# A two-layer recurrent trunk on one core: factors of a triangular inverse kept in half a PSUM bank, output transposes by two, sample states through the merge's banks

## The chip, the cores and the metric

The kernel runs on one core of a Trainium2 chip. The metric is the device time of one execution in microseconds. Five engines work beside one another: TensorE (PE in the profile: matmuls and transposes into PSUM; its weight loads are PEld), VectorE (DVE), ScalarE (ACT), GpSimd (POOL) and SyncE (SP, which here only issues DMAs). SBUF holds the tiles, PSUM has banks of 128 partitions by 512 floats, into which PE writes and from which DVE and ACT read.

## What is computed

A trunk of two layers over a prompt of 1024 tokens and 8 samples of 8 tokens, width 1024. Layer 0 is a gated linear recurrence, layer 1 a recurrence of the RWKV-7 kind with 16 heads of 64; each layer also attends to a memory, gates, projects back and adds to the residual. The part that the change touches is the recurrence of layer 1, whose reference is this step over time:

```python
def step(S, inp):
    r_t, w_t, k_t, v_t, a_t, b_t = inp
    sa = jnp.einsum('bhij,bhj->bhi', S, a_t)
    S = S * w_t[:, :, None, :] + sa[..., None] * b_t[:, :, None, :] + v_t[..., None] * k_t[:, :, None, :]
    y = jnp.einsum('bhij,bhj->bhi', S, r_t)
    return S, y
```

Its result is normalized by head, a bonus `(r*k).v` is added, and the prompt's and the samples' last states are outputs.

## The kernel before, in words

All arithmetic is in 32 bits. Up to about 1600 us of the profiled execution come layer 0, its output projection and the input projection of layer 1; from about 2170 us on the output projection of layer 1 runs. Between them lies the recurrence of layer 1.

It is computed in nine blocks: eight of 128 prompt tokens and one that holds the 64 tokens of all samples. `RSEQ` gives their order, 0, samples, 1, 2 ... 7. Each block is an object of class `Blk` with these stages:

- `pre` and `score_steps`: scaled keys (tiles `BKz`, `AR`; DVE and POOL), their products on PE (`psc`), masked by DVE into the tile `Q`.
- `tokens` and `values`: the keys turned by PE (`pbk`) and copied to `BKt`, and the value rows loaded.
- `inverse` (L1524 to L1562): within a block, tokens depend on one another through a unit triangular matrix of every head. ACT copies its diagonal parts of 16 by 16 to `Ld`, DVE transposes them (`Lu`) and adds two halves to the factors `L16` (L1549, the tile prints as `L`). Then fifteen steps of a substitution run on DVE, each a product `pd<-Xc,L` (L1553) of t by t elements in a partition and a sum `Xc<-pd` (L1554). Each step needs the one ahead of it. The result goes to `XN` and `XP`.
- `merge_steps` (L1564 to L1609): five rounds of 32 by 32 matmuls (`pn`, `px`, `py`, L1579) that put the inverses of 16 together to those of 64, with copies by DVE and ACT between them.
- `chain` (L1641 on): the recurrence itself. It starts from the state `S` (`chain<-S,AR`, L1669), goes through `W` and `UV`, and leaves the next state (`chainS`, L1719 to L1725). One block's chain needs the state of the one ahead.
- `out` (two groups `k`, each `out_group`, L1780 on): normalization by ACT, DVE and POOL, four transposes of `yv` on PE into one PSUM tile `pyt` (L1818), and copies with a bias to `oT` by ACT (L1821), then a DMA to `mixT`.
- `sample_in` for the samples' block: eight pairs of heads, each with a load of the states, transposes into PSUM (`ps`, L1621), a copy `S0T` (L1622), and two groups of sixteen products (`pas`, L1636) with a copy `AS` each (L1638). `sample_out` writes the samples' last states, two PSUM tiles a pair (`psn`, L1769, and `pec`, L1776).

The loop over the blocks says for block n: its chain; the merge of n+1 woven with the scores of n+2 (`WV` says how many steps of each in turn); the inverse and tokens of n+2; one or more pairs of `sample_out`; `pre` of n+3; `out` of n-1. Ahead of the loop two lists, `PLAN` and `PLAN2`, give the order of the last gate projections (g0 to g11), memory heads (x, s) and the first blocks' stages (p, c, t, i, m with a block's number). All this is a program order alone: a scheduler then places each instruction on its engine's queue by that order and its own simulated times, and adds the waits.

Three PSUM pools matter: two banks `psi` for the merge's tiles, one bank `psn` that `ps`, `pas`, `psn`, `pec` and `pyt` share one after the other, and three banks `psg` for the chain.

Of the kernel before, what the change touches and what calls it, by code (L numbers as in the profile page):

```python
# [9 lines left out]
F32 = mybir.dt.float32  # L10
F32R = mybir.dt.float32r
I32 = mybir.dt.int32
AF = mybir.ActivationFunctionType
# [30 lines left out]
    "x0 g0 x2 x1 g1 x3 s0 g2 g3 s1 g4 g7 p0 g5 c0 s2 s3", "t0 i0 m0 p1 g6 g8 g9 g10 g11")]  # L44
# [3 lines left out]
WV = (3, 8)  # L48
# [937 lines left out]
def rwkv_layer(ctx, g, nn, left):  # L986
# [252 lines left out]
    g.psi, g.psn = pool_ps("psinv", 2), pool_ps("pssmp", 1)  # L1239
    P["b"] = pS.enter_context(pool(g, "rb", 1))  # L1240
# [8 lines left out]
    with pool(g, "rl", 1, "right") as rl, pool(g, "sm2", 2, "right") as g.sm2:  # L1249
# [23 lines left out]
        for n, x in enumerate(seq):  # L1273
            if n == SIN:
                smp.sample_in()
            x.chain()
            ops(n + 1, "values")
# [106 lines left out]
class Blk:  # L1384
# [140 lines left out]
    def inverse(self):  # L1525
# [22 lines left out]
        L16 = self.tile("L16", "L16", 16, 16)  # L1548
# [61 lines left out]
    def sample_state(self, p):  # L1610
# [4 lines left out]
        ps = g.psn.tile([128, NB, 64], F32, name="ps0", tag="n")  # L1615
# [9 lines left out]
    def sample_in(self):  # L1625
# [4 lines left out]
        for p in range(8):  # L1630
            S0T = self.sample_state(p)
            o = HV[p // 4]
            for h in range(2):
                ps = g.psn.tile([128, 2, NB, LS], F32, name="pas", tag="n")
                for bb in range(NB):
                    nc.tensor.matmul(ps[o, :, bb, :], S0T[HV[h], bb, :], self.AR[p // 4][HV[h], p % 4, :2, LS * bb:LS * bb + LS],  # L1636
                                     start=True, stop=True)
                nc.scalar.activation(self.AS0[o, p % 4, h], ps[o].rearrange("p a b t -> p (a b t)"), AF.Copy)  # L1638
# [116 lines left out]
    def sample_out(self, pairs):  # L1755
# [3 lines left out]
        for p in pairs:  # L1759
# [4 lines left out]
            ps = g.psn.tile([128, NB, 64], F32, name="psn", tag="n")  # L1764
# [10 lines left out]
            ps = g.psn.tile([128, NB, 64], F32, name="pec", tag="n")  # L1775
# [9 lines left out]
    def out_group(self, k, last):  # L1785
# [30 lines left out]
        pt = g.psn.tile([128, 4, 128], F32, name="pyt", tag="n")  # L1816
        for j in range(4):
            nc.tensor.transpose(pt[:, j, :n], yv[:n, j], g.ident[:n, :n])  # L1818
        for j in range(4):
            for r, ts in halves:  # L1820
                nc.scalar.activation(oT[:, j, ts.start - self.t0:ts.stop - self.t0], pt[:, j, r], AF.Identity,  # L1821
                                     bias=vcol(g, "lb", 4 * k + j))
# [8 lines left out]
FILL = [[("x", 0)], [("x", 1)], [("x", 2)], [("x", 3), ("s", 0)], [("s", 1), ("s", 2), ("s", 3)], [("s", 4), ("s", 5), ("s", 6), ("s", 7)], [], [("g", 9), ("g", 8), ("g", 10), ("g", 11)]]  # L1831
# [39 lines left out]
```

## Time and profile before

| | us |
|---|---|
| median of 3 executions | 2331.82 |
| lowest and highest | 2329.45, 2335.67 |
| the profiled execution | 2339.18 |
| its span in the trace | 2337.4 |
| PE busy in the span | 2178.2 (93%) |
| DVE busy | 1326.3 (57%) |
| ACT busy | 1004.1 (43%) |
| POOL busy | 697.2 (30%) |

The profiled execution was 7.4 us longer than the median of the three others, and 1.8 us of it lie outside the span. A share over the whole span is a mean of stages with different limits. The views used below are cut to the stages: busy time by stretch, one line's durations, waits by engine, and the timeline.

### The profile page before, as it was taken

To read this page: it belongs to the slowest core of one execution; us is meant where nothing else is said; L and a number is where in the kernel's file an instruction comes from. 1 tells how busy PE (TensorE), PEld (TensorE's weight loads), DVE (VectorE), ACT (ScalarE), POOL (GpSimd) and SP (SyncE) were. 2 spreads that over 40 slices of the span, in tenths; PEclk is the share of its full clock that TensorE was granted. 3 is DMA by queue.
4 is the path that set the end of the run, shared out by engine and by line. 5 is a ranking of instruction groups with operands and counts; after the bars stand their busy time and mean duration, and the time that the engine had idled before them with its cause. 6 is when DMAs were issued, how large, how long until landed. Compare 5 with 4: busy or idle time off the path is not lost. (4 is left out here: it accounts for less than half of the span.)

```text
span 2337.4 us, 50528 instructions
## 1 busy us (share of the span) xinstructions
PE 2178.2 (93%) x20945; PEld 1956.6 (84%) x20945; DVE 1326.3 (57%) x2596; ACT 1004.1 (43%) x2244; POOL 697.2 (30%) x561
## 2 busy tenths in 40 slices
PE   5999999999999979989989999899999999998997
PEld 5989888887878858878979998898888888888786
DVE  6134666657776553375795313334666689875633
ACT  4223444444444442266554312444544545455411
POOL 3101122122122310044563412112233355546432
PEclk9999999999999989999989998999997799889999
DMA  5136122123431363215434424235432234314653
GB/s 188 62 101 172 49 73 66 46 63 102 115 94 57 101 218 115 76 48 198 151 132 156 126 95 138 60 81 152 123 113 76 58 90 117 94 52 126 188 156 100
DMA packets 360504, 253.00 MB, mean 108 GB/s; under 512 B 120570, under 2 KB 326594, under 8 KB 360274
## 3 DMA queue, kind: packets, MB, share of 16 engines
q1 hardware_dynamic: 348226, 237.66, 34.1%
q0 software_dynamic: 2544, 7.64, 1.0%
q10 hardware_dynamic: 9504, 4.46, 0.7%
q8 instruction: 165, 2.70, 0.5%
q14 instruction: 65, 0.53, 0.1%
HBM read 172.59 MB, written 77.11 MB: 107 GB/s over the span
## 5 line engine op out<-in xcount | busy, mean ns | idle before, releaser
L199 POOL TENSOR_TENSOR wlo<-wraw,whi 128x1024 fp32r<-128x1024 f32 (+1 forms) x88 | 199.0, 2269 | 569.7 <-ACT whi L196 532.7
L217 PE MATMUL pg<-hi,whi 128*128 128x288 f32 (+3 forms) x800 | 268.8, 336 | 3.4 <-DVE qk L611 3.3
L218 PE MATMUL pg<-lo,whi 128*128 128x288 f32 (+3 forms) x800 | 265.3, 332 | 0.0
L219 PE MATMUL pg<-hi,wlo 128*128 128x288 f32 (+3 forms) x800 | 262.4, 328 | 0.0
L196 ACT ACTIVATE whi<-wraw 128x1024 fp32r<-128x1024 f32 (+1 forms) x104 | 102.6, 993 | 162.6 <-issue 67.9
L217 PEld LDWEIGHTS pg<-hi,whi 128*128 128x128 f32 x800 | 153.2, 191 | 18.7 <-DVE qk L611 4.2
L218 PEld LDWEIGHTS pg<-lo,whi 128*128 128x128 f32 x800 | 153.2, 191 | 11.1 <-issue 1.6
L219 PEld LDWEIGHTS pg<-hi,wlo 128*128 128x128 f32 x800 | 152.9, 191 | 10.5 <-issue 1.0
L903 PE MATMUL pout<-owh,bh 128*128 128x512 f32 (+1 forms) x432 | 142.8, 399 | 13.0 <-ACT owh L196 13.0
L903 PE MATMUL pout<-owh,bl 128*128 128x512 f32 (+1 forms) x432 | 141.4, 396 | 2.1 <-DVE bl L199 2.1
L903 PE MATMUL pout<-owl,bh 128*128 128x512 f32 (+1 forms) x432 | 142.6, 396 | 0.0
L217 PE MATMUL pg<-xhi,whi 128*128 128x384 f32 (+2 forms) x392 | 128.0, 327 | 7.7 <-DVE evs L1147 5.0
L219 PE MATMUL pg<-xhi,wlo 128*128 128x384 f32 (+2 forms) x392 | 126.4, 322 | 0.0
L218 PE MATMUL pg<-xlo,whi 128*128 128x384 f32 (+2 forms) x392 | 125.7, 321 | 0.0
L903 PEld LDWEIGHTS pout<-owh,bh 128*128 128x128 f32 (+1 forms) x432 | 79.2, 184 | 33.9 <-ACT owh L196 13.2
L196 ACT ACTIVATE bh<-br 128x512 fp32r<-128x512 f32 (+1 forms) x54 | 32.1, 605 | 161.0 <-POOL br L872 75.2
L199 DVE TENSOR_TENSOR bl<-br,bh 128x512 fp32r<-128x512 f32 (+1 forms) x54 | 47.5, 880 | 94.0 <-ACT bh L196 94.0
L689 DVE TENSOR_TENSOR qk<-qk,tot 128x512 f32<-128x512 f32 (+1 forms) x96 | 83.0, 865 | 29.7 <-PE plev L717 18.5
L903 PEld LDWEIGHTS pout<-owh,bl 128*128 128x128 f32 (+1 forms) x432 | 79.1, 183 | 23.7 <-DVE bl L199 2.5
L243 PE MATMUL pg<-xhi,whi 128*128 128x384 f32 (+1 forms) x408 | 97.3, 335 | 0.0
L903 PEld LDWEIGHTS pout<-owl,bh 128*128 128x128 f32 (+1 forms) x432 | 79.3, 184 | 21.0 <-issue 0.4
L243 PE MATMUL pg<-xhi,wlo 128*128 128x384 f32 (+1 forms) x408 | 96.6, 334 | 0.0
(457 smaller groups left out, 6000.2 us busy)
## 6 DMA issues: line engine op xcount, KB each, us to landing
wraw<-in_w_in_dram SPq DMA_DIRECT2D x72, 512.0 KB
oraw<-in_w_out_dram SPq DMA_DIRECT2D x24, 512.0 KB
wraw<-in_w_mem_kv_dram SPq DMA_DIRECT2D x16, 512.0 KB
gT<-evs SPq DMA_DIRECT2D x12, 544.0 KB
vv<-vtk SPq DMA_DIRECT2D x24, 256.0 KB
br<-brT SPq DMA_DIRECT2D x24, 256.0 KB
gt<-gT SPq DMA_DIRECT2D x24, 256.0 KB
br<-mixT SPq DMA_DIRECT2D x24, 256.0 KB
```

Of the source, the lines that this page charges most:

```text
L196: nc.scalar.activation(hi, src, AF.Copy)
L199: (nc.gpsimd if elo == "pool" else nc.vector).tensor_sub(lo, src, hi.bitcast(F32))
L217: nc.tensor.matmul(out, ah, bh, start=first, stop=False)
L218: nc.tensor.matmul(out, ah, bl, start=False, stop=False)
L219: nc.tensor.matmul(out, al, bh, start=False, stop=last)
L243: nc.tensor.matmul(z[:, :n], a[:, k], x(k)[:, t0:t0 + n], start=first, stop=last)
L689: nc.vector.tensor_tensor(v, v, w[:, :, :, None].to_broadcast([128, 2, n // (2 * h), h]), op=ALU.mult)
L903: nc.tensor.matmul(ps[c][:p], a[:, k, :p], w[:, 512 * c:512 * c + 512], start=first, stop=last)
```

## The change

First, the factors `L16` are no longer a tile of SBUF. The pool `psn` of one bank becomes one tile for the whole stage, `g.half` of 128 by 512; its first 256 columns are `L16`. DVE's sum writes them into PSUM, and each product of the substitution reads one operand from there.

Second, the other 256 columns take the transposes of `out_group`: two at a time with their copies, then the next two, where it was four into a tile of a whole bank.

Third, the tiles of the samples' states (`ps`, `pas`, `psn`, `pec`) now come from `psi`, the two banks of the merge.

Fourth, the order: in `PLAN` gate g6 comes ahead of g5 and leaves `PLAN2`, where t0 goes behind m0; `WV` goes from 3 and 8 to 1 and 4; in the loop the next block's `values` go ahead of `sample_in` and the chain, and the chain is issued under a higher priority. The last table `FILL` changes its quotes alone.

```diff
-    "x0 g0 x2 x1 g1 x3 s0 g2 g3 s1 g4 g7 p0 g5 c0 s2 s3", "t0 i0 m0 p1 g6 g8 g9 g10 g11")]
+    "x0 g0 x2 x1 g1 x3 s0 g2 g3 s1 g4 g7 p0 g6 g5 c0 s2 s3", "i0 m0 t0 p1 g8 g9 g10 g11")]
-WV = (3, 8)
+WV = (1, 4)
...
     g.psi, g.psn = pool_ps("psinv", 2), pool_ps("pssmp", 1)
+
+    g.half = g.psn.tile([128, 512], F32, name="half", tag="n")
...
         for n, x in enumerate(seq):
+            ops(n + 1, "values")
             if n == SIN:
                 smp.sample_in()
-            x.chain()
-            ops(n + 1, "values")
+            with tc.high_priority():
+                x.chain()
...
-        L16 = self.tile("L16", "L16", 16, 16)
+        L16 = g.half[:, :256].rearrange("p (t s) -> p t s", s=16)
         nc.vector.tensor_add(L16[al], Lu[al, :, :16], Lu[al, :, 16:])
...
-        ps = g.psn.tile([128, NB, 64], F32, name="ps0", tag="n")
+        ps = g.psi.tile([128, NB, 64], F32, name="ps0", tag="i")
...
-                ps = g.psn.tile([128, 2, NB, LS], F32, name="pas", tag="n")
+                ps = g.psi.tile([128, 2, NB, LS], F32, name="pas", tag="i")
...
-            ps = g.psn.tile([128, NB, 64], F32, name="psn", tag="n")
+            ps = g.psi.tile([128, NB, 64], F32, name="psn", tag="i")
...
-            ps = g.psn.tile([128, NB, 64], F32, name="pec", tag="n")
+            ps = g.psi.tile([128, NB, 64], F32, name="pec", tag="i")
...
-        pt = g.psn.tile([128, 4, 128], F32, name="pyt", tag="n")
-        for j in range(4):
-            nc.tensor.transpose(pt[:, j, :n], yv[:n, j], g.ident[:n, :n])
-        for j in range(4):
-            for r, ts in halves:
-                nc.scalar.activation(oT[:, j, ts.start - self.t0:ts.stop - self.t0], pt[:, j, r], AF.Identity,
-                                     bias=vcol(g, "lb", 4 * k + j))
+        for z in range(0, 4, 2):
+            pt = g.half[:, 256:].rearrange("p (j t) -> p j t", j=2)
+            for j in range(2):
+                nc.tensor.transpose(pt[:, j, :n], yv[:n, z + j], g.ident[:n, :n])
+            for j in range(2):
+                for r, ts in halves:
+                    nc.scalar.activation(oT[:, z + j, ts.start - self.t0:ts.stop - self.t0], pt[:, j, r], AF.Identity,
+                                         bias=vcol(g, "lb", 4 * k + z + j))
```

The kernel after has the same number of instructions on each engine. Its queues read the same as before on every engine up to the part that `PLAN` orders; from there on they differ. In the code after, the lines of the second layer's blocks stand three further down (four from `out_group`'s transposes on): L1553 is L1556, L1818 is L1822. Three places show how the queues moved.

On DVE, in the sixth inverse (of block 4), from the product of six by six on: before, its steps stand among rows of the samples' output (`Sn`, `bx`, `de`), of the next scores (`Q`) and of the keys (`G`, `BKz`).

```order
L1770 TENSOR_TENSOR Sn<-psn,Sn 128x512
L1767 TENSOR_TENSOR bx<-BKt,blk 128x512
L1553 TENSOR_TENSOR pd<-Xc,L_20951 128x6x6
L1767 TENSOR_TENSOR bx<-BKt,blk 128x512
L1483 TENSOR_TENSOR Q<-psc,rm 128x512
L1434 SCALAR_TENSOR_TENSOR G<-smask,sg 128x512
L1554 TENSOR_REDUCE Xc<-pd 128x6
L1777 TENSOR_TENSOR Sn<-pec,Sn 128x512
L1773 TENSOR_TENSOR de<-id_18096,ec 128x512
L1553 TENSOR_TENSOR pd<-Xc,L_20951 128x7x7
L1444 TENSOR_TENSOR BKz_15091<-bb,sg 64x4x2x64 x2
L1483 TENSOR_TENSOR Q<-psc,rm 128x512
```

After, in the same inverse:

```order
L1556 TENSOR_TENSOR pd<-Xc,half 128x6x6
L1557 TENSOR_REDUCE Xc<-pd 128x6
L1556 TENSOR_TENSOR pd<-Xc,half 128x7x7
L1557 TENSOR_REDUCE Xc<-pd 128x7
L1556 TENSOR_TENSOR pd<-Xc,half 128x8x8
L1557 TENSOR_REDUCE Xc<-pd 128x8
L1556 TENSOR_TENSOR pd<-Xc,half 128x9x9
L1557 TENSOR_REDUCE Xc<-pd 128x9
L1705 COPY UV<-chain_18104 64x512
L1556 TENSOR_TENSOR pd<-Xc,half 128x10x10
L1557 TENSOR_REDUCE Xc<-pd 128x10
L1556 TENSOR_TENSOR pd<-Xc,half 128x11x11
```

The steps now follow one another. Between the factors and the last sum of the inverses that lie in the loop, the fifth to the eighth, 23, 34, 34 and 30 rows of other work stood before; 13, 14, 7 and 11 stand there now.

On PE, in the samples' stage (`pas` are the products with the samples' states, `ps` the transposes of the next pair; `psc` and `pbk` are scores and turned keys of other blocks; `pn` and `px` belong to a merge): before,

```order
L1480 MATMUL psc<-AR,BKz_15091 128x128 x5
L1636 MATMUL pas<-AR,S0T 64x2x8 x8
L1579 MATMUL pn_19197<-XN,Q 32x32 x16
L1579 MATMUL pn_19198<-XN,Q 32x32 x16
L1636 MATMUL pas<-AR,S0T 64x2x8 x8
L1666 MATMUL chain_18105<-ident,AS_18272 128x64
L1480 MATMUL psc<-AR,BKz_15091 128x128 x4
L1508 MATMUL pbk<-ident,BKz_15090 128x64 x8
L1579 MATMUL px_19233<-N1p,XP 32x32 x5
L1621 MATMUL ps_18533<-ident,Sn_18534 128x64 x4
L1621 MATMUL ps_18533<-ident,Sn_18541 128x64 x4
L1666 MATMUL chain_18105<-ident,AS_18272 128x64
```

and after:

```order
L1639 MATMUL pas<-AR,S0T 64x2x8 x16
L1511 MATMUL pbk<-ident,BKz_15090 128x64 x16
L1669 MATMUL chain_18104<-ident,AS_18277 128x64
L1624 MATMUL ps_18390<-ident,Sn_18391 128x64 x4
L1624 MATMUL ps_18390<-ident,Sn_18398 128x64 x4
L1669 MATMUL chain_18104<-ident,AS_18277 128x64
L1511 MATMUL pbk<-ident,BKz_15091 128x64 x16
L1639 MATMUL pas<-AR,S0T 64x2x8 x16
L1483 MATMUL psc<-AR,BKz_15090 128x128 x4
L1669 MATMUL chain_18104<-ident,AS_18277 128x64
L1624 MATMUL ps_18427<-ident,Sn_18428 128x64 x4
L1483 MATMUL psc<-AR,BKz_15090 128x128 x3
```

The merge's matmuls no longer stand between the pairs. The merge of the samples' block comes in one piece behind the eighth pair.

On PE, at the transposes of an out group inside the loop, with the semaphores on which a row waits (each named after the engine that raises it): before,

```order
L1508 MATMUL pbk<-ident,BKz_15091 128x64 x5
L1818 MATMUL pyt<-ident,yv 128x128 [waits PE_49]
L1818 MATMUL pyt<-ident,yv 128x128 x3
L1480 MATMUL psc<-AR,BKz_15090 128x128 [waits DVE_49,Pool_49]
L1480 MATMUL psc<-AR,BKz_15090 128x128 x2
L1579 MATMUL py_19307<-XP,N1p 32x32 [waits PE_49,Activation_49]
L1579 MATMUL py_19307<-XP,N1p 32x32 x3
```

and after:

```order
L1822 MATMUL half<-ident,yv 128x128 [waits DVE_49]
L1822 MATMUL half<-ident,yv 128x128
L1483 MATMUL psc<-AR,BKz_15091 128x128 [waits PE_49,Pool_49]
L1483 MATMUL psc<-AR,BKz_15091 128x128 x3
L1483 MATMUL psc<-AR,BKz_15091 128x128 [waits DVE_49]
L1483 MATMUL psc<-AR,BKz_15091 128x128 x3
L1582 MATMUL py_19355<-XP,N1p 32x32 [waits PE_49,Activation_49]
...
L1483 MATMUL psc<-AR,BKz_15091 128x128 [waits DVE_49]
L1483 MATMUL psc<-AR,BKz_15091 128x128 x3
L1822 MATMUL half<-ident,yv 128x128 [waits Activation_49]
L1822 MATMUL half<-ident,yv 128x128
```

The first pair of transposes now waits for DVE, which is the last product of the inverse two blocks on, since that reads the other half of the same bank; the second pair waits for ACT, the copies of the first pair. On DVE, the factors of the fifth to the seventh inverse (`half<-Lu`, L1552) wait for ACT in turn, the last copy of the out stage ahead of them.

## Rows read from the trace of the kernel before

**Rows 1.** Busy time of the engines in five stretches of the span (start:end in us, its length, then busy us and instructions of PE, PE weight loads, DVE, ACT and POOL, the granted clock as a share of the full one, the DMA engines' mean busy share and GB/s): the part that PLAN and PLAN2 order, the samples' stage, the blocks with an inverse of their own behind them, the last blocks, the output projection.

```profile
1600.00:1717.00 117.00, 108.66 (x1186) 101.89 (x1184) 64.09 (x136) 59.57 (x134) 23.91 (x23) 0.96 0.43 123
...
1755.00:1842.00 87.00, 84.49 (x1070) 78.87 (x1070) 56.14 (x114) 39.84 (x97) 32.01 (x28) 0.65 0.29 74
1842.00:2077.00 235.00, 222.67 (x3829) 196.20 (x3827) 198.74 (x365) 124.94 (x316) 125.42 (x127) 0.91 0.33 88
2077.00:2170.00 93.00, 86.19 (x1583) 80.14 (x1582) 59.09 (x115) 46.91 (x114) 51.77 (x51) 0.91 0.32 100
2170.00:2338.00 168.00, 151.25 (x655) 118.94 (x653) 71.25 (x115) 39.91 (x92) 61.11 (x39) 0.95 0.49 150
```

**Rows 2.** The products of the substitution alone (L1553, tile pd): busy us and instructions of DVE, then clock, DMA share and GB/s, in three stretches, which hold one, four and one inverse.

```profile
1730.00:1755.00 25.00, 5.31 (x15) 1.00 0.43 112
...
1842.00:2077.00 235.00, 31.39 (x60) 0.91 0.33 88
2077.00:2170.00 93.00, 7.28 (x15) 0.91 0.32 100
```

**Rows 3.** The same view for the sums of the substitution (L1554, tile Xc), the stretch with four inverses.

```profile
1842.00:2077.00 235.00, 14.09 (x60) 0.91 0.33 88
```

**Rows 4.** The timeline of DVE inside the sixth inverse (start us, us, engine, line, operation, tiles and shapes, count).

```profile
1948.65 0.27 DVE L1553 TENSOR_TENSOR pd<-Xc,L 128x121 f32<-128x121 f32 x1
1948.95 0.28 DVE L1554 TENSOR_REDUCE Xc<-pd 128x11 f32<-128x121 f32 x1
1949.27 1.10 DVE L1553 TENSOR_TENSOR pd<-Xc,L 128x144 f32<-128x144 f32 x1
...
1951.86 0.33 DVE L1553 TENSOR_TENSOR pd<-Xc,L 128x169 f32<-128x169 f32 x1
```

**Rows 5.** The timeline of POOL at the same time.

```profile
1948.94 1.26 POOL L1451 TENSOR_TENSOR AR<-r,G 128x512 f32<-128x512 f32 x1
```

**Rows 6.** All instructions of four DVE lines in the whole span (count: shortest/median/longest in ns, first and last start, forms): the products of the substitution, both inputs in SBUF, and three lines of two inputs of which one is a PSUM tile (pos, psc, chainS), the first of these with 128 elements in a partition.

```profile
L1553 DVE TENSOR_TENSOR pd<-Xc,L x135: 142/284/2268, 1669.0 to 2093.0; 128x1 f32<-128x1 f32 x8, 128x4 f32<-128x4 f32 x8, 128x9 f32<-128x9 f32 x8, 128x16 f32<-128x16 f32 x8
...
L427 DVE TENSOR_TENSOR oS<-oS,pos x8: 270/280/289, 578.0 to 1657.2; 128x128 f32<-128x128 f32 x8
...
L1483 DVE TENSOR_TENSOR Q<-psc,rm x64: 651/682/693, 1619.7 to 2070.8; 128x512 f32<-128x512 f32 x64
...
L1724 DVE TENSOR_TENSOR S<-chainS,S x30: 669/686/693, 1751.3 to 2168.1; 128x512 f32<-128x512 f32 x30
```

**Rows 7.** The longest waits of PE in 1842 to 2077 (engine and line, what it waited for: us in total, times, longest).

```profile
PE chain L1696 <- ACT W L1679: 2.2, 2, 1.9
PE psc L1480 <- DVE Q L1483: 1.9, 1, 1.9
```

**Rows 8.** PE's timeline in the samples' stage: sixteen products of a pair with its states (L1636) at two times, and the transposes of two pairs' states one after the other (L1621).

```profile
1740.41 1.10 PE L1636 MATMUL pas<-AR,S0T 64*64 64x16 f32 x16
...
1759.04 0.66 PE L1621 MATMUL ps<-ident,Sn 64*128 64x64 f32 x8
...
1768.91 1.89 PE L1636 MATMUL pas<-AR,S0T 64*64 64x16 f32 x16
...
1772.95 1.06 PE L1621 MATMUL ps<-ident,Sn 64*128 64x64 f32 x8
```

**Rows 9.** Busy time of the engines as in Rows 1, for three slices of the samples' stage.

```profile
1780.00:1800.00 20.00, 17.49 (x150) 16.24 (x149) 17.35 (x31) 7.31 (x16) 9.70 (x9) 0.76 0.45 119
1800.00:1820.00 20.00, 20.00 (x226) 18.49 (x225) 5.53 (x8) 6.19 (x16) 0.72 (x1) 0.50 0.11 28
1820.00:1840.00 20.00, 20.00 (x268) 18.57 (x267) 17.05 (x39) 9.89 (x24) 10.77 (x9) 0.55 0.34 84
```

**Rows 10.** What ACT waited for in 1755 to 1842 (as in Rows 7).

```profile
ACT AS L1638 <- PE pas L1636: 18.2, 9, 4.6
```

**Rows 11.** PE's timeline at the start of the loop: the first matmuls of the first block's merge, the last of the gate projections (pg) and the last of that merge.

```profile
1690.79 1.20 PE L1579 MATMUL pn<-XN,Q 32*32 32x32 f32 x64
...
1708.69 0.31 PE L219 MATMUL pg<-xhi,wlo 128*128 128x320 f32 x1
...
1715.00 1.78 PE L1579 MATMUL py<-Q,XM 32*32 32x32 f32 x32
```

**Rows 12.** All copies out of the transposes (L1821) in the whole span, as in Rows 6.

```profile
L1821 ACT ACTIVATE oT<-pyt,vec x104: 299/340/379, 1837.5 to 2193.5; 128x64 f32<-128x64 f32 x72, 128x128 f32<-128x128 f32 x32
```

**Rows 13.** PE's timeline: the first state products (chain<-S,AR, L1669) of four blocks one after the other.

```profile
1870.18 1.05 PE L1669 MATMUL chain<-S,AR 128*128 128x128 f32 x7
...
1919.61 1.01 PE L1669 MATMUL chain<-S,AR 128*128 128x128 f32 x3
...
1968.86 1.16 PE L1669 MATMUL chain<-S,AR 128*128 128x128 f32 x8
...
2023.90 1.16 PE L1669 MATMUL chain<-S,AR 128*128 128x128 f32 x8
```

**Rows 14.** The timeline of the sixth inverse, its factors (L1549) and its last sum (L1554) on DVE, and of the out stage that lies over it: its first transposes on PE (L1818), its last copies on ACT (L1821).

```profile
1924.85 0.42 DVE L1549 TENSOR_TENSOR L<-Lu 128x256 f32<-128x256 f32 x1
...
1959.08 0.37 DVE L1554 TENSOR_REDUCE Xc<-pd 128x15 f32<-128x225 f32 x1
...
1942.99 0.66 PE L1818 MATMUL pyt<-ident,yv 128*128 128x128 f32 x4
...
1964.65 1.75 ACT L1821 ACTIVATE oT<-pyt,vec 128x64 f32<-128x64 f32 x8
```

More of the change, by code (lines that the diff above doesn't have):

```diff
@@ L1827 @@
 HV = (slice(0, 64), slice(64, 128))
-FILL = [[("x", 0)], [("x", 1)], [("x", 2)], [("x", 3), ("s", 0)], [("s", 1), ("s", 2), ("s", 3)], [("s", 4), ("s", 5), ("s", 6), ("s", 7)], [], [("g", 9), ("g", 8), ("g", 10), ("g", 11)]]
+FILL = [[('x', 0)], [('x', 1)], [('x', 2)], [('x', 3), ('s', 0)], [('s', 1), ('s', 2), ('s', 3)], [('s', 4), ('s', 5), ('s', 6), ('s', 7)], [], [('g', 9), ('g', 8), ('g', 10), ('g', 11)]]
 SEQ = [8, 0, 1, 2, 3, 4, 5, 6, 7]
```

## The prediction

> **What bounds the kernel now.** I read the busy time by stretch first [rows 1]. In every stretch of the second layer's blocks PE is the engine with the least room: 222.7 of 235 us in the loop from 1842 to 2077, 84.5 of 87 in the samples' stage before it. [...] So PE could do the same work in less time: the loop has 12.3 us in which PE idles and some 20 us of lower clock (0.09 of 222.7), 32 us in all; the samples' stage, at the full clock, some 55 us of work (0.65 of 84.5) in a stretch of 87.
>
> In the loop DVE comes next, with 198.7 of 235 us (85%). The reader should ask what that busy time is made of. The products of the substitution take 31.4 us there [rows 2], the sums of the same steps 14.1 [rows 3]. The two do the same numbers of elements, and where a product runs undisturbed it takes what its sum takes, 0.27 beside 0.28 us at 11 by 11 [rows 4]. The next product, 12 by 12, takes 1.10 us, and just then POOL works on two SBUF inputs [rows 4, 5]; the one of 13 by 13 takes 0.33 again. So about 17.3 us of the loop's products (31.4 less 14.1) are time lost beside POOL, 4.3 an inverse. DVE operations of two inputs of which one lies in PSUM show none of that: 64 scores never took over 693 ns against a median of 682, and 30 state sums never over 693 [rows 6], in stretches in which POOL is busy for half of the time (125 of 235 us). The change puts one operand of each product into PSUM.
>
> **The change part by part.** Differences are worked out against the profiled execution, 2339.2 us with a span of 2337.4, and then taken off the median of 2331.8: both ran the same program, and what separates them is no part of the sum. The output projection behind the blocks has PE busy for 151 of 168 us and starts when the last block is through [rows 1], so time won before it goes to the end.
>
> *Factors in PSUM.* The instruction count stays. A product then has one PSUM input, a sum none. A small operation of that kind, 128 elements in a partition, takes 270 to 289 ns [rows 6], no more than a free product of 121 (0.27 us): the operand itself costs nothing, to within 0.02 us by 135, 3 us. What it saves in the loop is at most the 17.3 us, if the substitution is what all else waits for; at least nothing, if PE sets the pace anyway. PE's longest waits there name ACT's W and DVE's Q, 2.2 and 1.9 us [rows 7], small pieces, but DVE's queue carries Q, UV, N1p and the inverse together at 85%, and its rows in the order after are compact (13, 14, 7 and 11 rows of other work inside the four inverses for 23, 34, 34 and 30). PE's room of 32 us is enough to take it. I take two thirds, −11 us, since the higher end needs every collision to lie on the path. Outside the loop the last inverse wins 3.8 us of DVE time (7.3 less 3.5) in a stretch where DVE is at 64%: −1. The first stretches have DVE work to spare under PE: 0.
>
> [...]
>
> *The samples' states through two banks.* Before, ps, pas, psn and pec follow each other through one bank, and the next group waits until ACT has copied the last one out: ACT's own view shows it waiting 18.2 us for pas in nine pieces [rows 10], and one pair follows another after 13.9 us (1759.04 and 1772.95) [rows 8]. After, two banks alternate, and the order puts the pairs one behind the other with wide score products (psc) between them, where narrow 32 by 32 rows of a merge stood. What it is worth hangs on PE's clock. Sixteen products take 1.10 us at the full clock and 1.89 later [rows 8]; the slices show 0.76 where psc rows were many, then 0.50 and 0.55 with PE busy throughout [rows 9]. Bounds: at the full clock the stretch would need 55 us of PE and its 2.5 of idle, −29; at half clock throughout 110 us, +23. Wide rows between the pairs speak for a higher clock, the merge in one piece behind them against. I take a third of the way up, −10 us.
>
> *The samples' merge and the start of the loop.* The merge's tiles share the two banks with the samples' states, so it cannot start until the eighth pair is through; this is in the bounds above. The first block's merge had much cover before: its first matmuls at 1690.79, the last gate projection at 1708.69, its own end at 1716.8 [rows 11], so 18 of its 26 us lay among projections. In the order after, 27 projection matmuls follow its first row, where it was 76. Those 76 stood in 17.9 us with four rounds of the merge at 1.2 each among them, so some 0.17 us each (13.1 by 76), and 49 fewer are 8 us of cover less. Part of that work was moved and is not lost, but PE waits for the copies between the rounds: +4 (0 to +8).
>
> *Gates g6 and g5.* They move within a stretch in which PE idles for 8.3 of 117 us [rows 1]. 0, to within 3.
>
> *Transposes by two.* The copies stay 2 or 4 to a pair, 0.34 us each [rows 12]. The first pair now waits for the last product of the inverse two blocks on, the second for the copies of the first (two to four by 0.34, 0.7 to 1.4 us), and the next inverse's factors for the last copy. Behind a waiting transpose on PE stand scores and the merge's rounds, and the chain behind those. If the order puts them where these are done, the waits cost nothing; if the second pair is met too early in each of ten groups, 10 by 1.4, 14 us, and with waits for inverses 20. I take +3 (0 to +20).
>
> The sum: −11 −1 −10 +4 +0 +3 = −15. The profiled execution would go to 2324, the median to 2331.8 − 15 = 2317.
>
> **The rivals.** *A cycle through the shared bank, slower.* Inverse, transposes, next inverse now come one after the other, since the halves are one bank to the waits. Blocks follow one another in the loop after 49.4, 49.3 and 55.0 us, 51.3 in the mean [rows 13]. Before, the sixth inverse took 34.6 us (1924.85 to 1959.45) and the out stage over it 23.4 (1942.99 to 1966.40) [rows 14], and they overlapped by 16.5. If the inverse shrank only by its collisions (to 30.3) and the out stage stayed, they would need 53.7, with two handovers of 1 to 2 us some 57: 5 to 6 us a block too long, over five blocks +28. With the sample stage and the start as forecast (−10 +4 −1) that is +21, 2353 us. It decides from the point where inverse and out together pass 51 us a block. Against it: with so few other rows between its steps the inverse needs 7 us of its own and 5 to 10 for 7 to 14 others of up to 0.69 [rows 6].
>
> *The relief goes nowhere.* Either PE is the bound at 95%, or the products still collide, since their other input and their output stay in SBUF, so that the change doesn't do what it says. Then −11 and −1 drop out: −10 +4 +3 = −3, 2329 us. For it: PE's short waits on DVE [rows 7]. Against: the clean rows with one PSUM input [rows 6].
>
> *The half clock stays.* The samples' stage, with its merge pushed behind it, runs at half clock throughout: +23 in place of −10, sum +18, 2350 us. For it: the narrow products of the pairs now stand closer together; against: the same products at the full clock at 1740 [rows 8].
>
> *Both go all the way.* All 17.3 and 3.8 us come off the path and the samples' stage runs at the full clock: −17 −4 −29 = −50, 2282 us. For it: DVE at 85% in the loop, and PE's room of 32 us there; against: it needs every bound at its end.
>
> **How the numbers follow.** Forecast 2317 (its own range 2304 to 2326): 0.46. The relief goes nowhere, 2329: 0.20. All the way, 2282: 0.14. The cycle, 2353: 0.12. The half clock, 2350: 0.08. A difference of 0.3%, 7 us, is about what a measurement of this kernel tells from none, so faster means below 2325 and slower above 2339. Faster: 0.41 of the forecast, 0.14 and 0.05 of the idle relief, 0.60. Slower: 0.10 and 0.08 and 0.02, 0.20. The rest, 0.20, is the same. The range of 8 in 10 goes from 2287, which leaves out half of the case with 2282, to 2341, which leaves out most of the two slow ones.
>
> **What would show it.** In the profile after: products in the loop near 14 us instead of 31, with no maximum over 0.5 us, and inverses of 15 to 25 us instead of 35, are the first step; a clock above 0.65 and pairs less than 10 us apart in the samples' stage the second; PE waiting for DVE's last product or ACT's oT at the transposes for under 5 us in all the third. It is wrong if the loop's blocks still take 51 us with free products, if the transposes show up among PE's longest waits, or if the samples' merge at half clock holds up the chain.

## The result and the profile after

The change makes the kernel slower: 2345.98 us median (2345.27 to 2359.84, six runs) against 2331.34 before (2325.87 to 2337.96, six runs), a ratio of 1.0071 with a 95% interval of 1.0049 to 1.0093. 2317 was forecast, 15 us faster; it came out 15 us slower, outside the range of 2287 to 2341.

The profiled execution of the kernel after took 2345.34 us with a span of 2343.6, that of before 2339.18, 8 us above its median, so the two traces differ by 6 us where the medians differ by 15: what the traces are read for below explains at most these 6. Busy time by stretch, to read beside [rows 1] (same stretches, the last longer by the 6 us; columns as there):

```profile
1600.00:1717.00 117.00, 109.16 (x1127) 102.96 (x1128) 58.45 (x135) 58.55 (x134) 28.34 (x32) 0.93 0.44 127
1755.00:1842.00 87.00, 82.83 (x1101) 77.53 (x1102) 56.99 (x118) 40.73 (x97) 29.17 (x26) 0.71 0.31 80
1842.00:2077.00 235.00, 225.30 (x3794) 197.22 (x3791) 180.44 (x356) 121.76 (x311) 125.56 (x126) 0.91 0.32 85
2077.00:2170.00 93.00, 85.13 (x1578) 78.00 (x1577) 56.37 (x113) 47.24 (x116) 50.71 (x50) 0.89 0.34 103
2170.00:2344.00 174.00, 154.99 (x697) 120.18 (x695) 72.56 (x120) 42.35 (x95) 62.34 (x40) 0.97 0.47 144
```

The products of the substitution in two of these stretches, and all of them in the span, to read beside [rows 2, 6] (L1556 is L1553 of before):

```profile
1842.00:2077.00 235.00, 14.25 (x60) 0.91 0.32 85
2077.00:2170.00 93.00, 3.61 (x15) 0.89 0.34 103
```

```profile
L1556 DVE TENSOR_TENSOR pd<-Xc,half x135: 135/221/394, 1674.1 to 2097.7; 128x1 f32<-128x1 f32 x8, 128x4 f32<-128x4 f32 x8, 128x9 f32<-128x9 f32 x8, 128x16 f32<-128x16 f32 x8
```

The first sign of the forecast is there: 14.25 us for 31.39, the longest product 394 ns for 2268. DVE lost 18 us of work in the loop, and the sixth inverse took 21.8 us instead of 34.6. So is the second: the samples' stage shows a clock of 0.71 for 0.65, and its pairs follow each other after 9.9 us in the mean instead of 13.5. And the third: PE waited 0.7 us in all for the inverse's last product at the transposes, and not for their copies. Yet the loop went on at 52 us a block (state products at 1870.5, 1921.9, 1977.8, 2026.0 and 2078.0, against [rows 13] and 2077.1 for the fifth, 51.7 us a block), and the last product of the last chain ended at 2171.7 instead of 2167.7. Blocks of 51 us or more with free products were the forecast's own sign of being wrong. (The state products of [rows 13] are not each block's first, as their heading says, but the first of its second 64 tokens; the distance between blocks is the same. The one at 1870 is called the second state product below.)

Where the gain went is seen at the merges. From the first `pn` of a block's merge to its last `py`, by PE's trace, for the seven merges behind that of the samples:

| | first start, last end | inside merges | between them | from an inverse's end to its merge (fifth to eighth) |
|---|---|---|---|---|
| before | 1803, 2145 | 290 | 52 | 4, 4, 2, 7 |
| after | 1817, 2144 | 257 | 70 | 15, 10, 23, 16 |
| after, factors in SBUF, same queues (below) | 1818, 2167 | 280 | 70 | 13, 11, 23, 13 |

Before, the merges of these four blocks started 2 to 7 us after their inverses: there the inverses lay on the path. After, the merges are 33 us shorter in all, but they start 14 us later and stand 18 us further apart, so the last ends 1 us earlier only; and an inverse that is done waits 10 to 23 us for its merge. What stands there is seen on PE after the sixth inverse, which ended at 1945.2 (timeline of the kernel after; `psn` and `pec` are the samples' last states):

```profile
1945.26 1.02 PE L1772 MATMUL psn<-bx,UV 128*64 128x512 f32 x3
1946.22 1.12 PE L1779 MATMUL pec<-de,ones 128*128 128x512 f32 x2
...
1949.61 1.07 PE L1772 MATMUL psn<-bx,UV 128*64 128x512 f32 x2
...
1952.78 1.12 PE L1779 MATMUL pec<-de,ones 128*128 128x512 f32 x2
1953.84 1.15 PE L1713 MATMUL chain<-UV,Q 128*64 128x64 f32 x16
1954.91 1.19 PE L1582 MATMUL pn<-XN,Q 32*32 32x32 f32 x32
```

On DVE, in the same stretch:

```profile
1944.83 0.38 DVE L1557 TENSOR_REDUCE Xc<-pd 128x15 f32<-128x225 f32 x1
...
1946.32 0.69 DVE L1773 TENSOR_TENSOR Sn<-psn,Sn 128x512 f32<-128x512 f32 x1 [0.52 <-PE psn L1772]
...
1948.13 1.08 DVE L1563 STREAM_TRANSPOSE XN<-XI 128x512 f32<-128x512 f32 x1
...
1949.96 0.67 DVE L1780 TENSOR_TENSOR Sn<-pec,Sn 128x512 f32<-128x512 f32 x1
...
1953.43 0.69 DVE L1773 TENSOR_TENSOR Sn<-psn,Sn 128x512 f32<-128x512 f32 x1
```

Two pairs of last states go through the two banks, each tile read by DVE before its bank is written again, and only then comes the merge's `pn`: `XN`, which it reads, is done at 1949.2, the bank is read out at 1954.1, and `pn` starts at 1954.91. The kernel before, in the same block, had them inside a merge, between its rounds:

```profile
1928.11 1.13 PE L1776 MATMUL pec<-de,ones 128*128 128x512 f32 x2
...
1930.71 1.20 PE L1579 MATMUL py<-XP,N1p 32*32 32x32 f32 x64
1931.84 0.71 PE L1508 MATMUL pbk<-ident,BKz 64*128 64x64 f32 x8
1932.48 1.08 PE L1769 MATMUL psn<-bx,UV 128*64 128x512 f32 x4
```

PE's longest waits in the loop stay small, as in [rows 7]; an engine that is given other rows in its queue shows no wait:

```profile
PE chainS L1722 <- DVE UV L1705: 3.7, 2, 2.1
PE py L1582 <- ACT XM L1318: 2.2, 1, 2.2
PE psn L1772 <- DVE bx L1770: 1.6, 1, 1.6
```

### The profile page after: what moved, and what is told of

It reads as the page before. It is cut to its first block, busy times and chain, and to the rows that moved or that the text cites. A ratio compares the mean times of both kernels' runs of the same rounds, so it can differ in the third digit from the quotient of the medians.

```text
span 2343.6 us, 50542 instructions
## 1 busy us (share of the span) xinstructions
PE 2181.5 (93%) x20945; PEld 1956.7 (83%) x20945; DVE 1300.2 (55%) x2596; ACT 1003.6 (43%) x2244; POOL 695.6 (30%) x561
```

## The experiments

Eighteen kernels ran, each beside the kernel before on the same chip. Ratios to before are of five rounds, with the 95% interval in brackets; 0.1% is 2.3 us.

**The parts, one at a time.** Theory O: the new order costs the time. Theory B: the waits through shared banks do.

The order alone: the plans, `WV`, the values and the priority of the diff, nothing else. 

> The kernel before with the change of order alone (both plans, 1 and 4 steps in the weave, values ahead, the chain at a higher priority); all PSUM tiles as before. Theory O (the new order costs the time): about 2346 us, 15 above before, as the whole change. Theory B (the waits through shared banks cost it): no slower than before, 2322 to 2333.

 Measured 2358.46, 1.0120 [1.0081, 1.0158]: worse than the whole change.

The states alone: the four lines `g.psn.tile(... tag="n")` of `ps0`, `pas`, `psn`, `pec` to `g.psi.tile(... tag="i")`. 

> The kernel before with the samples' states (ps, pas, psn, pec) through the merge's two banks and nothing else changed; the transposes keep a bank of their own. Theory O: within 4 us of before. Theory B, if the sharing with the merge is the costly wait: 8 to 15 us slower; in the samples' stage the merge's matmuls then stand behind the eighth pair, as in the kernel after.

 Measured 2355.36, 1.0110 [1.0072, 1.0149].

All PSUM parts without the order. 

> The whole change without its order: factors in half a bank, transposes by two, states through the merge's banks, plans and weave as before. Theory O: products of the substitution at 3.6 us an inverse, and 0 to 8 us faster than before. Theory B: about 15 us slower, as the whole change.

 Measured 2338.63, 1.0043 [1.0018, 1.0069], with products of 3.6 us an inverse.

The whole change with

```diff
-        L16 = g.half[:, :256].rearrange("p (t s) -> p t s", s=16)
+        L16 = self.tile("L16", "L16", 16, 16)
```

> The whole change, but the factors stay in SBUF (the transposes by two keep their half bank, whose other half lies idle). The products lose time beside POOL again (some 7 us an inverse), but inverse and transposes no longer wait for each other. Theory O: 2346 us or up to 10 more. Theory B, if it is the wait between inverse and transposes: back to 2331 to 2336.

 Measured 2356.9, 1.0131 [1.0080, 1.0181].

Neither theory holds alone: the order and the states each cost more than the whole, though not by much more than the intervals, and factors in PSUM seem to take some of it back. So the forecast's gain may be there, under two losses.

**Is it PE's time in the merge?** In the traces a merge matmul is followed by the next after some 17 ns where two tiles take turns and 36 ns where one runs alone (means over the two granted clocks that the traces of before and after show, 1.00 and 0.50 of the full one; at 1.00 16 and 32, at 0.50 27 and 53); the shared banks leave more of them alone. Theory M makes this the loss. The edit keeps the turns on PE's queue, without a wait:

```diff
                 for u in range(16):
-                    for c, z in zs:
-                        nc.tensor.matmul(z[out(*c), u], lhs(u, *c), rhs(u, *c), start=True, stop=True)
+                    for i, (c, z) in enumerate(zs):
+                        mm = nc.tensor.matmul(z[out(*c), u], lhs(u, *c), rhs(u, *c), start=True, stop=True)
+                        if len(zs) > 1 and u + i:
+                            g.tc.keep_in_program_order(mm)
```

In the whole change: 

> The whole change, and the merge's matmuls of two tiles held in turn on PE's queue (an order edge from each to the next, no wait added). In the traces so far a merge matmul is followed by the next one after some 17 ns where two tiles take turns and some 36 ns where one tile runs alone, and the kernels with more rows alone are the slower ones: starts of merge matmuls to the next start add up to 117 us before, 131 after, 135 with the states moved alone. Theory M (PE sets the pace, and the shared banks cost what the merge loses by running tile by tile): merge time near 70 us, 2346 less 40 to 60, so 2286 to 2306. Theory B (the waits through the banks themselves cost it): merge time falls, the total stays within 10 us of 2346, since PE then waits for the second bank.

 Measured 2347.29, 1.0065 [1.0040, 1.0090]: unchanged. In the kernel before: 

> The kernel before with the same order edges in the merge. Theory M: merge time from 117 to near 70 us, 2331 less 35 to 50, so 2281 to 2296; then it and the whole change with edges differ by less than 8 us or the change is ahead. Theory B: 0 to 10 us faster, and still 10 to 15 ahead of the whole change with edges.

 Measured 2336.38, 1.0015 [0.9996, 1.0034]. In the PSUM parts without the order: 

> Factors in half a bank, transposes by two and states through the merge's banks, order as before, with the order edges in the merge. Theory M: 2338 less 35 to 55, 2283 to 2303, ahead of the kernel before with edges by the 8 us that the samples' stage wins and a part of the 11 of the factors. Theory B: within 10 us of 2338.

 Measured 2340.67, 1.0024 [1.0008, 1.0040].

The edit did what it should: the merge matmuls, start to next start with no gap counted for more than 0.4 us, went from 117 to 95 us in the kernel before, from 131 to 102 in the one after. From the first chain product to the last, the kernel before without and with it (busy time as in [rows 1]; the second execution was 10 us above its kernel's median, the first 8):

```profile
1721.00:2168.00 447.00, 424.71 (x6904) 384.24 (x6904) 342.26 (x644) 224.55 (x555) 223.80 (x222) 0.86 0.33 90
```

```profile
1725.00:2174.00 449.00, 404.96 (x6890) 357.82 (x6890) 340.92 (x644) 224.73 (x562) 220.56 (x219) 0.86 0.33 90
```

PE is busy for 20 us less, and the stretch is as long as it was: theory M falls, and with it the reading of PE's 95% as its limit. The same stretch of the whole change with turns shows 403.66 of 455 us, at a clock of 0.82 instead of 0.87 (426.56 of 450 without). Over all its executions the median clock of the whole change goes from 0.945 to 0.9415 with turns, that of the PSUM parts without the order from 0.9495 to 0.9445, that of the kernel before stays at 0.947.

A kernel meant for the other end, the merge's two banks as one tile of two in the kernel before (`psi` one buffer, `tile([128, 2, 16, 32])`, its halves for the two quarters): 

> The kernel before with the two tiles of a merge's round taken as one tile of two banks; in its order nearly every merge matmul stands behind one of its own tile (1813 of 1904 rows, 996 before), and all else is as before. Theory M: merge time up by some 30 us (817 rows of two matmuls by 18 ns), so 2331 plus 20 to 35. Rival: the merge's time is hidden behind waits for DVE, 2331 plus 0 to 8.

 The expectation misread the queue: the halves of one tile print under one name, and by the trace they took turns (87 us from start to start). So it is no test of rows alone. It measured 2320.37, 0.9938 [0.9915, 0.9961], the only kernel here that beats before, and it beats the change too. In the stretch PE is busy for 382 of 430 us at a clock of 0.90:

```profile
1725.00:2155.00 430.00, 382.44 (x6895) 341.79 (x6894) 338.53 (x643) 225.61 (x564) 218.16 (x220) 0.90 0.35 94
```

Why it gains where the turns alone do not is open. Its clock differs too: over its six executions the median granted clock is 0.9535, beside 0.947 for the kernel before on the same chip.

What the clock goes with can be estimated from the kernel before alone: its 93 executions beside these runs all have the same work and the same queues, and 0.001 less of mean granted clock goes with 1.7 us more (clocks of 0.941 to 0.955, correlation −0.83). By that estimate some 11 of the 14 us of this kernel go with its clock. Whether the clock brings the time or follows from it, the estimate does not say.

**Which states, and which piece of the order.** Only `ps` and `pas` moved: 

> The kernel before with only the samples' first states (ps, pas) through the merge's two banks; psn, pec and the transposes keep the bank of before. With all four moved, the second state product stood 7 us earlier (1863 against 1870), and the rest of the blocks took 20 us longer. Theory L (the last states, psn and pec, take the merge's banks from it in the loop): 5 to 10 us faster than before, the loop from the second block on in 287 to 292 us. Rival E (the first states push the merges back, and the loop pays for it later): 10 to 20 us slower.

 Measured 2343.91, 1.0049 [1.0030, 1.0069]. Only `psn` and `pec`: 

> The kernel before with only the samples' last states (psn, pec) through the merge's banks. Theory L: 15 to 25 us slower than before, the loop from the second block on in 300 to 310 us with DVE waiting for pn some 18 us as with all four moved (5.6 before). Rival E: within 5 us of before.

 Measured 2346.47, 1.0059 [1.0039, 1.0079]. Both cost, and together they make the 1.0110 of all four. The first comes out as rival E has it and against theory L; the second is against rival E, and just short of theory L's range, but L's sign is missing: DVE waits 6.1 us for `pn`, where before it waits 5.6 and 18.1 with all four moved. The last states do stand in front of the merges: in that kernel the fifth to eighth inverse wait 27, 20, 14 and 7 us for their merges, against 4, 4, 2 and 7 before and 3, 4, 9 and 7 with only the first states moved. `in_only` also refutes the forecast's picture (PE's timeline of that kernel: the last `pas`, the samples' merge behind them, and the second state product):

```profile
1778.77 2.53 PE L1636 MATMUL pas<-AR,S0T 64*64 64x16 f32 x26
1781.23 4.08 PE L1480 MATMUL psc<-AR,BKz 128*128 128x128 f32 x16
1785.24 2.15 PE L1579 MATMUL pn<-XN,Q 32*32 32x32 f32 x64
...
1868.15 1.06 PE L1669 MATMUL chain<-S,AR 128*128 128x128 f32 x8
```

The pairs are done at 1781 instead of 1828, 47 us earlier; the samples' merge starts at 1785 instead of 1755, because it must wait for them; and the second state product comes at 1868 instead of 1870. Then the blocks take 310 us to the end of the last chain product, where they took 298, with the same tiles as before.

Only `with tc.high_priority():` around the chain: 

> The kernel before with only the chain issued at a higher priority. The order alone cost 27 us. Theory P (the chain ahead of the merges' rounds and inverses on every queue holds up what the next chain needs): 15 to 25 us slower. Rival: the plans and the weave cost it, and this is within 6 us of before.

 Measured 2343.58, 1.0045 [1.0024, 1.0066], some 10 us, between the two expectations; the plans, the weave and the values were not run alone, and make the rest of the order's 28 if the pieces add up.

The PSUM parts, old order, and one tile of two banks: 

> Factors in half a bank, transposes by two and states through the merge's banks, order as before, and the merge's two banks given out as one tile of two, as in the kernel that was 0.6% faster than before (in which, by its trace, merge matmuls took turns after all: 87 us from start to start, 117 before; the two halves of one tile print under one name). A tile of samples' states then takes both banks. Theory T (one tile of two banks makes the rounds go through in one piece, and that is worth some 12 us in any setting): 2338 less 8 to 15. Rival L: the states now exclude a whole round, so slower than 2338 by 5 to 20.

 Measured 2362.59, 1.0123 [1.0097, 1.0150]. One tile of two banks won 14 us in the kernel before and loses 19 here. A state's tile now shuts out a whole round; that this is the reason is argued.

**With the queues held.** A relief cannot be told from the order that comes with it as long as each edit lets the scheduler lay all queues anew. So the next kernels hold every engine's queue in a given order, by an edge of order from each instruction to the next; edges add no wait.

```diff
+            if prev is not None and i.engine == prev.engine:
+                tc.add_manual_dep(i, prev.name, mybir.DependencyInfo(mybir.DependencyClass.NoSync, mybir.DependencyReason.DATA),
+                                  reason="pin")
+            prev = i
```

The whole change's order, factors in SBUF: 

> The whole change with its factors in SBUF as in the run of that name, but every engine's queue held, by edges of order alone, in exactly the order of the whole change. The only difference from the whole change is where the factors lie. Theory A (collisions beside POOL are on the path, the order did the rest): slower than 2346 by 5 to 15 us, products of the substitution at 5 to 9 us an inverse. Rival N (the relief goes nowhere, and the 11 us between the whole change and the one with factors in SBUF came from another order): within 4 us of 2346.

 Measured 2368.81, 1.0156 [1.0131, 1.0180], against 1.0071 for the whole change. The order without the diff's fourth part, factors in SBUF: 

> The same with the order of before's plans: the run without the change of order (2339) with its factors back in SBUF and every queue held in that run's order. Theory A: 2344 to 2354. Rival N: within 4 us of 2339.

 Measured 2361.57, 1.0124 [1.0098, 1.0149], against 1.0043. On every engine the held queues read in the traces as those of the kernel that they are compared with. The relief is worth 0.85% and 0.81%, 19 to 20 us where 12 were forecast; both runs are slower than their expectations had it. Its products, to read beside L1556 above, and the stretch of the chains, to read beside the 450 us of the whole change:

```profile
L1555 DVE TENSOR_TENSOR pd<-Xc,L x135: 138/275/2105, 1676.2 to 2120.1; 128x1 f32<-128x1 f32 x8, 128x4 f32<-128x4 f32 x8, 128x9 f32<-128x9 f32 x8, 128x16 f32<-128x16 f32 x8
```

```profile
1725.00:2195.00 470.00, 443.21 (x6927) 399.95 (x6926) 345.26 (x645) 225.65 (x559) 223.43 (x220) 0.83 0.31 85
```

By the table above its merges take 280 us where the whole change has 257, with the same 70 us between them and the same waits of 11 to 23 us behind the inverses: what the relief wins in the loop it wins inside the merges. How is not shown. One way is that their copies `N1p` stand behind the products on DVE. Another is PE's clock: for the same matmuls PE is busy for 443 us in this stretch where the whole change has 427, at 0.83 for 0.87, and the longest piece of it lies in the first merge behind the samples' (busy time as above, the whole change and then this kernel):

```profile
1817.00:1853.00 36.00, 31.57 (x625) 29.78 (x623) 23.38 (x56) 21.90 (x55) 7.48 (x7) 0.87 0.06 16
```

```profile
1818.00:1862.00 44.00, 40.40 (x628) 38.06 (x626) 27.12 (x60) 24.20 (x61) 7.48 (x7) 0.66 0.04 9
```

Over all executions the two kernels with factors in SBUF have median clocks of 0.937 and 0.9405, their partners 0.945 and 0.9495; by the estimate above 13 to 15 of the 19 to 20 us go with that.

`in_only`, held in before's order from the last copy `AS` on: 

> The samples' first states through the merge's two banks, as in the run that was 12 us slower than before, but from the last of their copies on every engine's queue is held in the order of the kernel before. Tiles and work are those of that run. Theory R (a scheduler's order that was fitted to the kernel before is lost with any change to what it sees, and that is the cost): the blocks from the second state product to the last take 298 us as before where that run took 309, and the total is 2324 to 2336. Rival W (the sharing of banks costs it): 2340 to 2348.

 Measured 2337.38, 1.0008 [0.9988, 1.0027], with 296.5 us from the second state product to the last chain product, as before (297.5), where `in_only` had 309.9. The first states' new banks cost nothing and win nothing, to within 6 us; the 11 us that they cost alone were the order behind them.

A swap of two equal halves in the kernel before, `for h in range(2)` to `for h in (1, 0)` in the last states, which changes no tile, bank or amount of work: 

> The kernel before, in which the two heads of a pair are issued in the other order in the samples' last states: same tiles, banks, work and waits, but the scheduler's order moves on every engine (some 1100 rows of difference on PE). Theory R: slower than before by 4 to 20 us. Rival W: within 4 us of before.

 Measured 2337.58, 1.0020 [1.0001, 1.0038]. This new order by itself costs some 5 us, 0 to 9 by the interval, at the low end of what theory R expected and not clear of rival W: hardly free, but far from 25.

**Off the merge's banks.** Factors, half bank and transposes by two kept, first states in the merge's banks, but the last states in two halves of four samples through the other half bank. 

> Factors in half a bank, transposes by two, the samples' first states through the merge's banks, but their last states (psn, pec) in two halves of four samples through the other half bank instead of the merge's banks; plans, weave and priority as before. It adds sixteen matmul groups and sixteen DVE operations of half the size. By the parts measured: 2332, less 22 for the factors, plus 4 to 12 for an order that nobody fitted, plus up to 8 for the half bank that now has the transposes and the last states behind each inverse: 2314 to 2330. Rival (the waits for the half bank, one after the other, cost more than the merge's banks did): 2338 to 2350, no better than without this.

 Measured 2419.43, 1.0365 [1.0334, 1.0395]. The same with the merge's banks as one tile: 

> The same with the merge's two banks given out as one tile of two, which made the kernel before 13 us faster and the one with all states in the merge's banks 24 us slower. Theory (it helps as long as the last states stay out of these banks): 2305 to 2325. Rival (a first state that takes both banks holds up the merges as much as a last one): 2340 to 2360.

 Measured 2390.92, 1.0250 [1.0223, 1.0277]. Both come out on the rivals' side, and slower than even those had it. In the first of the two, the last product of an inverse on DVE and the state behind it on PE:

```profile
2032.32 0.39 DVE L1554 TENSOR_TENSOR pd<-Xc,half 128x225 f32<-128x225 f32 x1
```

```profile
2032.76 1.12 PE L1772 MATMUL half<-bx,UV 128*64 128x256 f32 x4 [1.48 <-DVE pd L1554]
2034.41 1.12 PE L1772 MATMUL half<-bx,UV 128*64 128x256 f32 x4 [0.53 <-DVE Sn L1773]
```

The states start 0.05 us after the inverse lets the bank go (2032.71). A cycle through the shared bank, the prediction's first rival, is seen here, where more goes through it: from 1870 to 2170 DVE waits 34 us for PE at this bank and PE 10 us for DVE, and the blocks in the loop take 64 to 76 us instead of 51. How much of the 85 us is the cycle, and how much the added operations, the new order or a clock of 0.93 (0.947 before), is not told apart.

## Why the prediction was wrong

The sum can be measured as a chain of steps, each by its ratio: states to the merge's banks +1.10%; half bank and transposes by two, factors still in SBUF, to 1.0124, +0.14%; factors to PSUM, to 1.0043, −0.81%; the diff's order, to 1.0071, +0.28%. In us of before: +26, +3, −19, +7, together +17 against 15 by the medians. Each step has an uncertainty of 8 to 11 us, and all but the third include a new order of all queues.

- **Factors in PSUM, −11 −1: the collisions went as forecast, the term was too small.** −19 to −20 with the order held, where two thirds of the loop's collisions were taken: the 17.3 us there and the 3.8 behind come to 21. That the measured gain is near this may be luck, since by the estimate from the kernel before 13 to 15 us of it go with a higher clock of PE, which the term did not have. The rival that the relief goes nowhere is refuted. The operand in PSUM shows no price: sixty products take 14.25 us in the loop of the kernel after, the sixty sums of the same steps 14.22, some 3.6 us an inverse each.
- **The samples' states through two banks, −10: the step that failed, +26.** It failed twice. The first states' wait for one bank was taken for the limit of the samples' stage; PE filled it with other work, so 47 us of earlier pairs moved the next block by 2. Alone these states cost 11 us, and nothing once the order behind them is held. The clock on which the −10 hung did rise, from 0.65 to 0.71, but not where wide score rows were put between the pairs: from 1755 to 1780 it is 0.64, for 0.73 before. And the last states, which the change moves in the same way, were not priced at all: alone they cost 14 us. The banks that they take are those of the merge, which starts where its inverse ends; in the kernel after they stand between the two. That their banks and not only their order cost the 14 us is argued from the timelines, not shown: with two banks the order of before, which had a merge's two tiles and a state in PSUM at once, cannot be held.
- **Transposes by two, +3: +3 measured**, with the half bank and a new order, and uncertain by 11 us, so the agreement says little. That the price is low because little goes through the bank is argued.
- **Start of the loop and gates, +4 +0: the order as a whole measured +7** on top of the PSUM parts and +28 on the kernel before. The rival of the half clock did not come: the samples' stage shows a clock of 0.71, above the 0.65 of before. The prediction priced the places it had looked at and took the rest of a new order for free. `in_only`, `priority_only` and the swap show some 5 to 11 us for orders in which no work and no later resource changed.
- **PE as the bound, behind the rivals and the 32 us of room**: refuted, as far as PE's amount of work goes, by the runs with turns. 20 us less of it returned as idle time. How fast PE runs is another matter: a lower clock goes with a longer time, 1.7 us for each 0.001 in the kernel before. Of the 32 us, 12.3 are idle time and 20 the author's estimate from the clock of 0.91 in [rows 1], as the 55 us of the samples' stage are one from its 0.65. They take PE's time as inverse to the clock; the merge's matmuls took 53 ns at 0.50 for 32 at 1.00, 1.7 times as long.

The two slower rivals, 2353 and 2350, lie near the measured 2346 by their numbers, but not by their paths: inverse and transposes cost each other next to nothing, and the clock did not fall in the samples' stage. A cycle through a shared bank may be right in kind; then it is the other bank, that of merge and last states.

## What to carry to other kernels

If tiles are moved into a bank of a stage that starts where the critical work ends, ask who stands in front of that stage in the queue after, not only which wait is removed elsewhere; and every tile that moves has to be in the sum. Where a scheduler lays all queues anew with each edit, a relief is measured by holding the queues and changing the resource alone; the granted clock of both runs belongs beside the times. An engine that is 95% busy is shown to be the bound only when work is taken from it and the stretch gets shorter.

## What the runs showed of the hardware

The 135 products of the substitution, DVE operations of two inputs with 1 to 225 elements in a partition, took at most 394 ns with one operand in PSUM, and the sixty in the loop took 14.25 us for 14.22 of the sums, while POOL was busy for 125.6 of 235 us. With the same queues and the operand in SBUF single ones took up to 2105 ns.

The merge's 32 by 32 matmuls followed each other after 16 ns where two tiles took turns, and after 32 ns in one tile, at a granted clock of 1.00 (27 and 53 ns at 0.50; kernels before and after). With turns the stretch of the chains did not get shorter: 449 us for 447 in the kernel before with 404.96 us of PE for 424.71, 455 for 450 in the whole change with 403.66 for 426.56. In the second the stretch's granted clock was 0.82 instead of 0.87, in the first 0.86 both times.

Among 93 executions of the kernel before, with granted clocks of 0.941 to 0.955, the time went with the clock: 1.7 us more for each 0.001 less (correlation −0.83).
